# Expert tiles between the scores split one product early, look-up tables on ScalarE, the last V tiles in other buffers, and the output by halves

## The chip, the cores and the metric

The kernel runs on one core of a Trainium2 chip. The metric is the device time of one execution in microseconds. Work is done by five engines that each run their own instructions in order: TensorE (matrix products), VectorE, ScalarE, GpSimd and SyncE (which issues most of the DMAs).

## The reference, cut to what matters

One encoder layer over 512 tokens of width 1024. The part around the change is the expert layer (PEER) and the final norm:

```python
q = (ht @ w_q).reshape(T, PEER_HEADS, 2, PEER_HALF_DIM)
s1 = jnp.einsum('thd,hkd->thk', q[:, :, 0], keys[:, 0])
s2 = jnp.einsum('thd,hkd->thk', q[:, :, 1], keys[:, 1])
v1, i1 = lax.top_k(s1, PEER_TOPK)          # 16 of 128 keys, in each half
v2, i2 = lax.top_k(s2, PEER_TOPK)
cand = (v1[..., :, None] + v2[..., None, :]).reshape(T, PEER_HEADS, 256)
sc, ci = lax.top_k(cand, PEER_TOPK)
idx = i1[ci // 16] * 128 + i2[ci % 16]     # look-ups along the last axis
gates = jax.nn.softmax(sc, axis=-1)
...
a = einsum('chkd,cd->chk', U[idx], h2)     # 16384 experts, 8 heads x 16 each
w = gelu(a) * gates
x = x + gate2 * einsum('chk,chkd->cd', w, V[idx])
return rmsnorm(x, g_final)
```

Before it come the adaLN modulation, attention, a gated MLP and their output projection, which the change doesn't touch.

## The kernel before

Tokens lie in four blocks of 128. For blocks 0 to 2 (384 tokens) the experts are computed densely: the 16384 experts are 128 tiles of 128, tile e gives a 128 x 384 product with U (`a_mm`, 24 products into one accumulator, then Gelu in `a_gelu`), is multiplied with a gate matrix, and goes into six accumulators `outs` (three blocks by two halves of 512 columns) with 18 products. Block 3 (`GB`) is computed by gathering its experts' rows; its route and its gathers are a list `fill` of small steps that is spread over the main loop by costs written beside them.

A float32 product is made of three products of split operands (`mm3`): each weight is split into a high part on ScalarE and a low part on VectorE (`split_into`, lines 77 and 78). `a_load` loads and splits an expert tile: raw tiles in the three buffers tagged `ur`, high and low parts in two each, `uh` and `ul`. V tiles use two buffers `vr` and two each of `vh` and `vl`; the last two tiles' parts already lie in `uh` and `ul`.

The stages around the change, in order of time:

- **Scores and routing** (from about 270 us). For each of eight heads `score` makes two query products and their key scores (`q`, `qT`, `sc`, `s`). Then come the expert tiles of that head (one each, nine behind the last), and then VectorE's key search of the head (`route_keys`). After each four heads a group is routed: `route_cands`, `route_pick`, `route_decode`, and two times `route_lookup`, which finds `i1[ci // 16]` and `i2[ci % 16]` without a gather: a one-hot mask of 12 x 16 x 16 values by a comparison (line 593), times the table of indices (line 595), summed by halves (lines 597 and 599).
- **Gate build** (about 467 to 608 us). For 48 steps of eight tokens, one-hot matrices are made on VectorE and ScalarE, multiplied on TensorE (`gg`), and stored. The order of TensorE, ScalarE and VectorE is written out by hand (`manual_schedule`), and twelve expert tiles (18 to 29) are woven in through the list `todo`.
- **Main loop** over e = 0 to 127. The U product runs `AHEAD` = 30 tiles ahead of the V product. The V products of the last four tiles (`TAIL`) are held and done together.
- **Output.** For each block: times `gate2`, plus the residual, sum of squares (ScalarE's Square), times `g_final`, root on GpSimd, scale on ScalarE, and two DMAs from SyncE's queue. Its tiles `yf` share the tag `ur`.

Outside the parts written by hand the framework's planner fixes the order of each engine's instructions before the run: what comes first in the program has precedence, and what is ready by its own estimate may go ahead of what is not. A tile waits for a buffer of its tag. So loads and small steps can stand far from their place in the program.

Of the kernel before, what the change touches and what calls it, by code (L numbers as in the profile page):

```python
# [9 lines left out]
F32 = mybir.dt.float32  # L10
F32R = mybir.dt.float32r
BF16 = mybir.dt.bfloat16
# [7 lines left out]
P = 128  # L20
# [37 lines left out]
def tile_kernel(ctx: ExitStack, tc: tile.TileContext, a: dict, out: bass.AP):  # L58
# [506 lines left out]
    def route_decode(r):  # L565
        pl, tag, ci = r["pl"], r["tag"], r["ci"]
        n = r["nb"] * r["nh"]
        rt_ = lambda m, dt=F32: pl.tile([P, n, K], dt, name=f"{m}{tag}", tag=m, bufs=1)
        t3, t2 = rt_("t3", U32), rt_("t2", U32)
        nc.vector.tensor_single_scalar(t3, ci, 3, op=ALU.logical_shift_right)  # L570
        nc.vector.tensor_single_scalar(t2, ci, 2, op=ALU.logical_shift_right)
        row, st, u = rt_("row"), rt_("rst"), rt_("ru")
        rcf = pl.tile([P, 2, n, K], BF16, name=f"rcf{tag}", tag="rcf", bufs=1)
        nc.vector.scalar_tensor_tensor(row, t3, 5.0, t2, op0=ALU.add, op1=ALU.max)
        nc.vector.scalar_tensor_tensor(row, row, 42.0, ci, op0=ALU.add, op1=ALU.max)
        nc.vector.tensor_scalar(row, row, -48.0, 0.0, op0=ALU.add, op1=ALU.max)
        nc.vector.tensor_copy(rcf[:, 0], row)
        nc.vector.tensor_scalar(st, row, 7.0, 8.0, op0=ALU.mult, op1=ALU.add)
        nc.vector.tensor_scalar(u, row, 3.0, 24.0, op0=ALU.mult, op1=ALU.add)
        nc.vector.scalar_tensor_tensor(st, row, 15.0, st, op0=ALU.mult, op1=ALU.min)  # L580
        nc.vector.scalar_tensor_tensor(st, u, 48.0, st, op0=ALU.min, op1=ALU.min)
        nc.vector.tensor_add(st, st, row)
        nc.vector.tensor_sub(rcf[:, 1], ci, st)
        i12f = pl.tile([P, n, 2, K], BF16, name=f"i12f{tag}", tag="i12f", bufs=1)
        nc.vector.tensor_copy(i12f, r["i12"].rearrange("p b h f k -> p (b h) f k"))
        r["rcf"], r["i12f"] = rcf, i12f

    def route_lookup(r, f, dst):

        n = r["nb"] * r["nh"]  # L590
        sh = [P, n, K, K]
        oh = r["pl"].tile(sh, BF16, name=f"oh{r['tag']}{f}", tag="oh", bufs=2)
        nc.vector.tensor_tensor(oh, r["rcf"][:, f].unsqueeze(2).to_broadcast(sh),
                                jrep.unsqueeze(1).to_broadcast(sh), op=ALU.is_equal)
        nc.vector.tensor_tensor(oh, oh, r["i12f"][:, :, f, :].unsqueeze(3).to_broadcast(sh), op=ALU.mult)
        for w in (8, 4, 2):
            nc.vector.tensor_add(oh[:, :, :w, :], oh[:, :, :w, :], oh[:, :, w:2 * w, :])
        o5 = oh.rearrange("p (b h) j k -> p b h j k", h=r["nh"])
        nc.vector.tensor_add(dst, o5[:, :, :, 0, :], o5[:, :, :, 1, :])
# [13 lines left out]
    with ExitStack() as qs:  # L613
# [78 lines left out]
        ahead = FIRST  # L692
        score(0)
        r = None
        for h in range(PH):
            if h + 1 < PH:
                score(h + 1)
            while ahead < FIRST + h + 1 + (LATE if h == PH - 1 else 0):
                dense_a(ahead)
                ahead += 1  # L700
            s_sb = scores.pop(h)
            hl = h % HG
            if hl == 0:
                r = route_tiles(R, f"d{h}", ND, HG)
            for b in range(ND):
                for f in range(2):
                    route_keys(r, b, hl, f, s_sb[:, b, f, :])
            if hl == HG - 1:
                hs = slice(h - HG + 1, h + 1)
                route_cands(r)  # L710
                for b in range(ND):
                    for i in range(HG):
                        route_pick(r, b, i, sca[:, b, h - HG + 1 + i, :])
                route_decode(r)
                for f, dst in ((0, i1a), (1, i2a)):
                    route_lookup(r, f, dst[:, :, hs, :])
        route_gates(R, sca, gts, ND * PH)

    flat = lambda t, b: t.rearrange("p b h k -> p b (h k)")[:, b, :]
# [3 lines left out]
    with ExitStack() as gs:  # L723
# [63 lines left out]
        for k in range(nu):  # L787
            e = ahead + k
            s0 = k * NG // nu
            st = {}  # L790
            todo[s0].append(lambda e=e, st=st: st.update(hl=a_load(e)))
            for c in range(KD):
                def part(e=e, st=st, c=c):
                    if c == 0:
                        st["p"] = a_psum(e)
                    a_mm(e, st["p"], st["hl"], c)
                todo[s0 + 2 + c * NG // nu // KD].append(part)
            todo[s0 + 3 + NG // nu].append(lambda e=e, st=st: a_gelu(e, st["p"]))
# [66 lines left out]
    for h in range(PH):  # L865
        for f in range(2):
            fill.append((1.6, lambda h=h, f=f: route_keys(st["r"], 0, h, f, st["sg"][:, 2 * h + f, :])))
    fill.append((1.2, lambda: route_cands(st["r"])))
    for h in range(PH):
        fill.append((1.3, lambda h=h: route_pick(st["r"], 0, h, st["sc"][:, 0, h, :])))  # L870
    fill.append((4.0, lambda: route_decode(st["r"])))
    for f in range(2):
        fill.append((5.0, lambda f=f: route_lookup(st["r"], f, st["i"][f])))
    fill.append((1.2, lambda: route_gates(st["R"], st["sc"], gtg, PH)))
    fill.append((0.3, gb_idx))
    for n in range(NS):
# [11 lines left out]
    for e in range(NE):  # L888
        if e + AHEAD < NE:
            dense_a(e + AHEAD)  # L890
        if e == 0:
            gt = g0
        elif e % GE == 0:
            gt = wp.tile([P, NTC, GE, TC], F32, name=f"g{e}", tag="g", bufs=2)
            nc.sync.dma_start(gt, gd[e // GE])
        vraw = vp.tile([P, D], F32, name=f"v{e}r", tag="vr", bufs=2)
        nc.sync.dma_start(vraw, a["peer_v"][e * P:(e + 1) * P, :])
        if e < NE - 2:
            vh = vp.tile([P, D], F32R, name=f"v{e}h", tag="vh", bufs=2)
            vl = vp.tile([P, D], F32R, name=f"v{e}l", tag="vl", bufs=2)  # L900
        else:
            vh = up.tile([P, D], F32R, name=f"v{e}h", tag="uh", bufs=2)
            vl = up.tile([P, D], F32R, name=f"v{e}l", tag="ul", bufs=2)
        nc.scalar.copy(vh, vraw)
        last = nc.vector.tensor_sub(vl, vraw, vh.bitcast(F32))
        w = a_tiles.pop(e)
        wv3 = w.rearrange("p (c t) -> p c t", t=TC)
        nc.vector.tensor_tensor(wv3, wv3, gt[:, :, e % GE, :], op=ALU.mult)  # L908
        wh = wp.tile([P, TD], F32R, name=f"w{e}h", tag="wh", bufs=TAIL)
        wl = wp.tile([P, TD], F32R, name=f"w{e}l", tag="wl", bufs=TAIL)  # L910
        split_into(wh, wl, w)
        held.append((e, wh, wl, vh, vl))
        if e < NE - TAIL or e == NE - 1:
            for b in range(ND):
                bs = slice(b * P, (b + 1) * P)
                for e_, wh, wl, vh, vl in held:
                    for hf in range(2):
                        sl = slice(hf * 512, (hf + 1) * 512)
                        mm3(outs[2 * b + hf], (wh[:, bs], wl[:, bs]), (vh[:, sl], vl[:, sl]),
                            e_ == 0, e_ == NE - 1)  # L920
            held.clear()
        due += slack[e] * rate
        with tc.issue_after(last.ins):
            while fill and (due >= fill[0][0] or e == NE - 1):
                cost, fn = fill.pop(0)
                fn()
                due -= cost
# [2 lines left out]

    gfin = gp.tile([P, D], F32, name="gfin", tag="g", bufs=4)
    nc.sync.dma_start(gfin, a["g_final"].partition_broadcast(P))
    for b in (GB, 0, 1, 2):
        if b in (GB, 0):
            xr = gp.tile([P, D], F32, name=f"xr{b}", tag="g", bufs=4)
        else:
# [1 line left out]
        nc.sync.dma_start(xr, x2d[b * P:(b + 1) * P, :])  # L938
        y = up.tile([P, D], F32, name=f"yf{b}", tag="ur", bufs=3)
        ss = gp.tile([P, 2], F32, name=f"ssf{b}", tag="ssf", bufs=2)  # L940
        for hf in range(2):
            sl = slice(hf * 512, (hf + 1) * 512)
            nc.vector.tensor_mul(y[:, sl], accg[:, sl] if b == GB else outs[2 * b + hf], gate2[:, sl])
            nc.vector.tensor_add(y[:, sl], y[:, sl], xr[:, sl])
            nc.scalar.activation(xr[:, sl], y[:, sl], AF.Square, accum_out=ss[:, hf:hf + 1])
            nc.vector.tensor_mul(y[:, sl], y[:, sl], gfin[:, sl])
        nc.vector.tensor_add(ss[:, 0:1], ss[:, 0:1], ss[:, 1:2])
        r = rstd_of(ss[:, 0:1], D, f"fin{b}")
        for hf in range(2):
            sl = slice(hf * 512, (hf + 1) * 512)  # L950
            nc.scalar.activation(y[:, sl], y[:, sl], AF.Copy, scale=r[:, 0:1])
            nc.sync.dma_start(out[b * P:(b + 1) * P, sl], y[:, sl])


def arrays_of(i):
# [59 lines left out]
```

## Time and profile before

| | us |
|---|---|
| median of 3 runs | 1567.22 (1566.68 to 1567.84) |
| the profiled execution, its own time | 1570.06 |
| its span, first to last instruction | 1568.3 |
| TensorE busy | 1492.6 |
| VectorE busy | 1240.9 |
| ScalarE busy | 636.6 |
| mean granted clock of TensorE, share of full | 0.981 |

The span is what the profile shows; the execution's own time has the 1.76 us around it too. Busy times overlap, since the engines work side by side. In the profile PE is TensorE's products, PEld its weight loads, DVE is VectorE, ACT ScalarE, POOL GpSimd, SP SyncE; a q behind a name is that engine's queue, and L595 is line 595 of the kernel.

### The profile page before, as it was taken

To read this page: it belongs to the slowest core of one execution; us is meant where nothing else is said; L and a number is where in the kernel's file an instruction comes from. 1 tells how busy PE (TensorE), PEld (TensorE's weight loads), DVE (VectorE), ACT (ScalarE), POOL (GpSimd) and SP (SyncE) were. 2 spreads that over 40 slices of the span, in tenths; PEclk is the share of its full clock that TensorE was granted. 3 is DMA by queue.
4 is the path that set the end of the run, shared out by engine and by line. 5 is a ranking of instruction groups with operands and counts; after the bars stand their busy time and mean duration, and the time that the engine had idled before them with its cause. 6 is when DMAs were issued, how large, how long until landed. Compare 5 with 4: busy or idle time off the path is not lost.

```text
span 1568.3 us, 21451 instructions
## 1 busy us (share of the span) xinstructions
PE 1492.6 (95%) x7675; PEld 1317.9 (84%) x7675; DVE 1240.9 (79%) x2388; ACT 636.6 (41%) x1092; POOL 397.1 (25%) x335
## 2 busy tenths in 40 slices
PE   2899999998979999999999999999999999999996
PEld 1765787887879999999999999999999999998884
DVE  6937865579989997987887878878888888886774
ACT  2533434432338997334333333333333333332343
POOL 1202100000000000002554444444544544542210
PEclk9899999999999999999999999999999999999998
DMA  9626334331325769666999999988999998987873
GB/s 366 232 79 223 130 132 148 112 104 48 101 94 159 237 211 300 218 224 220 354 351 319 321 330 328 326 318 318 336 330 314 326 325 315 333 287 230 256 237 121
DMA packets 147226, 380.71 MB, mean 243 GB/s; under 512 B 11184, under 2 KB 59840, under 8 KB 146864
## 3 DMA queue, kind: packets, MB, share of 16 engines
q1 hardware_dynamic: 103472, 221.02, 40.5%
q0 software_dynamic: 42352, 153.62, 28.7%
q10 hardware_dynamic: 1296, 4.72, 0.8%
q8 instruction: 60, 0.98, 0.2%
q14 instruction: 46, 0.38, 0.1%
HBM read 349.16 MB, written 30.15 MB: 242 GB/s over the span
## 4 chain that ended last, share of the span: by engine, by line
PE 86%; DVE 7%; DMA 3%; ACT 1%; issue 1%; POOL 0%; SPq 0%; ACTq 0%; POOLq 0%; DVEq 0%
PE out L83 11%; PE out L84 11%; PE out L82 11%; PE pa L82 11%; PE pa L84 11%; PE pa L83 11%; PE gg L770 5%; DMA wada<-w_ada 2%; PE q L82 1%; PE q L84 1%; PE q L83 1%; PE yo L82 1%; PE yo L84 1%; PE yo L83 1%; DVE macc L149 1%
## 5 line engine op out<-in xcount | busy, mean ns | idle before, releaser
L842 POOL DMA_INDIRECT gu<-peer_u,idx x128 | 181.3, 1417 | 653.6 <-DVE w17l L78 467.6
L842 POOL DMA_INDIRECT gv<-peer_v,idx x128 | 173.0, 1351 | 235.0 <-DVE accg L862 209.0
L850 DVE SCALAR_TENSOR_TENSOR scr<-gu,h2g 128x1024 bf16<-128x1024 f32 x128 | 156.5, 1222 | 24.1 <-DMA gu<-peer_u,idx 21.8
L862 DVE SCALAR_TENSOR_TENSOR accg<-gv,wg,accg 128x1024 f32<-128x1024 f32 x127 | 162.8, 1282 | 7.1 <-DMA gv<-peer_v,idx 4.6
L770 PE MATMUL gg<-o,o 128*128 128x128 f32 x768 | 96.0, 280 | 3.6 <-ACT o L764 2.0
L770 PEld LDWEIGHTS gg<-o,o 128*128 128x128 f32 x768 | 94.6, 196 | 4.1 <-ACT o L764 4.1
L908 DVE TENSOR_TENSOR a<-a,g 128x384 f32<-128x384 f32 x128 | 69.1, 550 | 6.4 <-DMA g<-gd 2.9
L764 ACT ACTIVATE o<-o1b,gT 128x128 f32<-128x128 bf16 x192 | 63.4, 405 | 13.8 <-DVE o1b L751 7.2
L518 ACT ACTIVATE a<-pa 128x384 f32<-128x384 f32 x128 | 61.7, 483 | 13.2 <-PE pa L84 13.2
L149 DVE SCALAR_TENSOR_TENSOR macc<-wada,csil,macc 128x1024 f32<-128x1024 f32 x40 | 51.2, 1280 | 9.5 <-DMA wada<-w_ada 9.1
L753 DVE TENSOR_TENSOR o<-iota_s,gT 128x1024 f32<-128x1024 f32 x48 | 58.4, 1216 | 0.3 <-PE gg L770 0.2
L757 DVE TENSOR_SCALAR o<-iota_s,gT 128x128 f32<-128x128 f32 x192 | 53.2, 339 | 0.0
L779 ACT COPY st<-gg 128x512 f32<-128x512 f32 x96 | 50.5, 581 | 0.0
L159 PE MATMUL mcol<-ident_s,macc 128*128 128x128 f32 x32 | 7.4, 391 | 26.6 <-DVE macc L146 23.1
L135 POOL DMA_DIRECT2D wada<-w_ada x32 | 17.1, 535 | 59.9 <-DVE macc L149 24.3
L159 PEld LDWEIGHTS mcol<-ident_s,macc 128*128 128x128 f32 x32 | 5.5, 201 | 28.3 <-DVE macc L146 17.9
L424 ACT ACTIVATE pe<-s,mx 128x512 f32<-128x512 f32 x16 | 11.0, 688 | 28.4 <-DVE mx L422 20.8
L684 PE MATMUL sc<-keys_s,qT 128*128 128x128 f32 x128 | 18.1, 284 | 2.8 <-ACT qT L681 2.8
L751 DVE TENSOR_TENSOR o1b<-erep,gB 128x512 bf16<-128x512 bf16 x48 | 20.0, 416 | 0.9 <-ACT gB L734 0.9
L684 PEld LDWEIGHTS sc<-keys_s,qT 128*128 128x128 f32 x128 | 15.6, 191 | 5.7 <-ACT qT L681 4.3
L531 DVE MAX8 v12d<-s 128x8 f32<-128x128 f32 x48 | 12.7, 280 | 9.4 <-ACT s L686 9.4
L431 PEld LDWEIGHTS o<-vv,pts 128*128 128x128 f32 x128 | 16.1, 192 | 2.3 <-DVE mx L422 0.8
(2789 smaller groups left out, 4952.2 us busy)
## 6 DMA issues: line engine op xcount, KB each, us to landing
gd<-st SPq DMA_DIRECT2D x12, 1984.0 KB, 7.9
g<-gd SPq DMA_DIRECT2D x31, 768.0 KB, 8.4
wada<-w_ada POOLq DMA_DIRECT2D x32, 512.0 KB, 4.7
wada<-w_ada SPq DMA_DIRECT2D x16, 512.0 KB, 10.1
x<-x SPq DMA_DIRECT2D x4, 512.0 KB, 12.4
x<-x ACTq DMA_DIRECT2D x4, 512.0 KB, 3.8
x2d<-x ACTq DMA_DIRECT2D x4, 512.0 KB, 2.8
gu<-peer_u,idx POOLq DMA_INDIRECT x128, 7.3
```

The lines of the kernel that those rows point to most:

```text
L82: nc.tensor.matmul(o, lhsT=lh, rhs=rh, start=first, stop=False)
L83: nc.tensor.matmul(o, lhsT=lh, rhs=rl, start=False, stop=False)
L84: nc.tensor.matmul(o, lhsT=ll, rhs=rh, start=False, stop=last)
L149: nc.vector.scalar_tensor_tensor(acc, w, csil[:, c:c + 1], acc, op0=ALU.mult, op1=ALU.add)
L518: nc.scalar.activation(t, p[:, :TD], AF.Gelu)
L753: nc.vector.tensor_tensor(o2s[n], iota.unsqueeze(1).to_broadcast([P, UT, P]), tT[:, 1, t0:t0 + UT].unsqueeze(2).to_broadcast([P, UT, P]), ...
L764: nc.scalar.activation(o1s[n][:, i, :], e[:, :, i], AF.Copy, scale=tT[:, 2, t0 + i:t0 + i + 1])
L770: nc.tensor.matmul(pgs[n][i // 4][:, i % 4 * P:(i % 4 + 1) * P], lhsT=o2[:, i, :], rhs=o1[:, i, :], start=True, stop=True)
L842: nc.gpsimd.indirect_dma_start(out=g, out_offset=None, in_=src, in_offset=bass.IndirectOffsetOnAxis(ap=idx[:, s:s + 1], axis=0))
L850: nc.vector.scalar_tensor_tensor(scr, g, 1.0, st["h2g"], op0=ALU.mult, op1=ALU.mult, accum_out=actg[:, n:n + 1])
L862: nc.vector.scalar_tensor_tensor(accg, g, wg[:, s:s + 1], accg, op0=ALU.mult, op1=ALU.add)
L908: nc.vector.tensor_tensor(wv3, wv3, gt[:, :, e % GE, :], op=ALU.mult)
```

## The change

Four edits in one.

- *Expert tiles.* The loop between the scores loads and splits tile e + 1 right behind the products of tile e, before that tile's Gelu and before the key search. The first tile of the gate build (18) is so loaded and split in the routing stage.
- *Look-up tables.* The cast of the indices to bf16 moves from VectorE to ScalarE (`route_tables`). `route_rep` makes on ScalarE a dense copy of the index table, repeated 16 times along the last axis, and the multiply reads this copy in place of the broadcast. There is one buffer for the copy and, instead of two, one for the mask. The costs in `fill` are adapted.
- *Last V tiles.* The raw tiles of e = 125, 126 and 127 take the tag `ur`.
- *Output.* The held products of a block finish its first half before its second. The output works by halves in an order written by hand for blocks 0 to 2: one half is multiplied by `g_final` into a tile `yg` ahead of the root and scaled by ScalarE, the other gets root and gain in one VectorE operation, and each half has its own queue, ScalarE's and SyncE's.

```diff
+    def route_tables(r):
         i12f = pl.tile([P, n, 2, K], BF16, name=f"i12f{tag}", tag="i12f", bufs=1)
-        nc.vector.tensor_copy(i12f, r["i12"].rearrange("p b h f k -> p (b h) f k"))
-        r["rcf"], r["i12f"] = rcf, i12f
+        nc.scalar.copy(i12f, r["i12"].rearrange("p b h f k -> p (b h) f k"))
+    def route_rep(r, f):
+        n = r["nb"] * r["nh"]
+        t = r["pl"].tile([P, n, K, K], BF16, name=f"rep{r['tag']}{f}", tag="rep", bufs=1)
+        nc.scalar.copy(t, r["i12f"][:, :, f, :].unsqueeze(3).to_broadcast([P, n, K, K]))
+        r["rep"][f] = t
...
-        oh = r["pl"].tile(sh, BF16, name=f"oh{r['tag']}{f}", tag="oh", bufs=2)
+        oh = r["pl"].tile(sh, BF16, name=f"oh{r['tag']}{f}", tag="oh", bufs=1)
...
-        nc.vector.tensor_tensor(oh, oh, r["i12f"][:, :, f, :].unsqueeze(3).to_broadcast(sh), op=ALU.mult)
+        nc.vector.tensor_tensor(oh, oh, r["rep"].pop(f), op=ALU.mult)
...
+        nxt = a_load(ahead)
...
-                dense_a(ahead)
+                hl, nxt = nxt, None
+                p = a_psum(ahead)
+                for c in range(KD):
+                    a_mm(ahead, p, hl, c)
+                nxt = a_load(ahead + 1)
+                a_gelu(ahead, p)
...
+                route_tables(r)
+                route_rep(r, 0)
                 route_cands(r)
...
-                for f, dst in ((0, i1a), (1, i2a)):
-                    route_lookup(r, f, dst[:, :, hs, :])
+                route_lookup(r, 0, i1a[:, :, hs, :])
+                route_rep(r, 1)
+                route_lookup(r, 1, i2a[:, :, hs, :])
...
-            todo[s0].append(lambda e=e, st=st: st.update(hl=a_load(e)))
+            if k:
+                todo[s0].append(lambda e=e, st=st: st.update(hl=a_load(e)))
+            else:
+                st.update(hl=nxt)
...
+    fill.append((0.0, lambda: (route_tables(st["r"]), route_rep(st["r"], 0))))
...
-    fill.append((4.0, lambda: route_decode(st["r"])))
-    for f in range(2):
-        fill.append((5.0, lambda f=f: route_lookup(st["r"], f, st["i"][f])))
+    fill.append((3.6, lambda: route_decode(st["r"])))
+    fill.append((4.0, lambda: route_lookup(st["r"], 0, st["i"][0])))
+    fill.append((0.0, lambda: route_rep(st["r"], 1)))
+    fill.append((4.0, lambda: route_lookup(st["r"], 1, st["i"][1])))
...
-        vraw = vp.tile([P, D], F32, name=f"v{e}r", tag="vr", bufs=2)
+        if e < NE - 3:
+            vraw = vp.tile([P, D], F32, name=f"v{e}r", tag="vr", bufs=2)
+        else:
+            vraw = up.tile([P, D], F32, name=f"v{e}r", tag="ur", bufs=3)
...
-                for e_, wh, wl, vh, vl in held:
-                    for hf in range(2):
-                        sl = slice(hf * 512, (hf + 1) * 512)
-                        mm3(outs[2 * b + hf], (wh[:, bs], wl[:, bs]), (vh[:, sl], vl[:, sl]),
-                            e_ == 0, e_ == NE - 1)
+                for hf, (e_, wh, wl, vh, vl) in [(hf, h) for hf in range(2) for h in held]:
+                    sl = slice(hf * 512, (hf + 1) * 512)
+                    mm3(outs[2 * b + hf], (wh[:, bs], wl[:, bs]), (vh[:, sl], vl[:, sl]),
+                        e_ == 0, e_ == NE - 1)
...
+    def o_sum(b, hf):
+        (xr, y, ss, yg), sl = outp[b], halves[hf]
+        nc.vector.tensor_mul(y[:, sl], accg[:, sl] if b == GB else outs[2 * b + hf], gate2[:, sl])
+        nc.vector.tensor_add(y[:, sl], y[:, sl], xr[:, sl])
+        nc.scalar.activation(xr[:, sl], y[:, sl], AF.Square, accum_out=ss[:, hf:hf + 1])
+
+    def o_gain(b):
+        xr, y, ss, yg = outp[b]
+        nc.vector.tensor_mul(yg, y[:, halves[0]], gfin[:, halves[0]])
...
+    def o_store(b):
+        (xr, y, ss, yg), r = outp[b], rs[b][:, 0:1]
+        nc.scalar.activation(yg, yg, AF.Copy, scale=r)
+        nc.vector.scalar_tensor_tensor(y[:, halves[1]], y[:, halves[1]], r, gfin[:, halves[1]],
+                                       op0=ALU.mult, op1=ALU.mult)
+        nc.scalar.dma_start(out[b * P:(b + 1) * P, halves[0]], yg)
+        nc.sync.dma_start(out[b * P:(b + 1) * P, halves[1]], y[:, halves[1]])
...
+    with tc.manual_schedule(engines={nc.vector.engine, nc.scalar.engine}):
+        for b in range(ND):
+            o_sum(b, 0)
+            if b:
+                o_store(b - 1)
+            o_gain(b)
+            o_sum(b, 1)
+            o_root(b)
+        o_store(ND - 1)
```

## Rows read from the trace of the kernel before

**Rows 1.** The page's first part: busy time, share of the span and instructions of each engine.
```profile
PE 1492.6 (95%) x7675; PEld 1317.9 (84%) x7675; DVE 1240.9 (79%) x2388; ACT 636.6 (41%) x1092; POOL 397.1 (25%) x335
```

**Rows 2.** Stretches: busy us (instructions) per engine, PEclk the granted clock, DMA share, GB/s.
```profile
368.00:384.00 16.00, 12.21 (x66) 10.28 (x65) 16.00 (x22) 4.83 (x10) 0.00 (x0) 1.00 0.03 9
384.00:400.00 16.00, 13.40 (x54) 10.39 (x54) 15.22 (x88) 3.57 (x6) 0.00 (x0) 0.89 0.10 34
...
448.00:464.00 16.00, 13.72 (x63) 13.72 (x64) 13.12 (x14) 1.93 (x3) 0.00 (x0) 0.79 0.30 98
...
520.00:560.00 40.00, 40.00 (x312) 40.00 (x311) 39.21 (x90) 36.89 (x96) 0.00 (x0) 1.00 0.76 234
...
1200.00:1400.00 200.00, 200.00 (x1005) 182.06 (x1004) 164.43 (x163) 69.42 (x96) 95.06 (x67) 1.00 0.90 321
```

**Rows 3.** Waits of TensorE, 256 to 482 us: us in total, times, longest us.
```profile
PE q L84 <- DVE wq12l L78: 2.8, 1, 2.8
PE sc L684 <- ACT qT L681: 2.8, 2, 1.4
```

**Rows 4.** The tiles of the two look-ups: xcount, ns min/median/max, first and last start, forms.
```profile
L593 DVE TENSOR_TENSOR ohd<-rcfd,jrep x4: 1746/1748/1752, 369.2 to 453.2; 128x3072 bf16<-128x3072 bf16 x4
L595 DVE TENSOR_TENSOR ohd<-ohd,i12fd x4: 3346/3348/3350, 371.1 to 459.5; 128x3072 bf16<-128x3072 bf16 x4
...
L585 DVE CAST i12fd<-i12d x2: 352/352/352, 354.2 to 438.2; 128x384 bf16<-128x384 uint32 x2
```

**Rows 5.** Timeline of ScalarE: start us, us, engine line op out<-in xcount [idle before <-releaser].
```profile
342.90 1.05 ACT L77 CAST wq9h<-wq9r 128x1024 fp32r<-128x1024 f32 x1 [4.60 <-PE q L83]
343.86 0.58 ACT L681 COPY qT<-q 128x512 f32<-128x512 f32 x1
```

**Rows 6.** Timeline where the last head's scores arrive and the gate build starts, VectorE, then TensorE.
```profile
416.64 0.49 DVE L531 MAX8 v12d<-s 128x8 f32<-128x128 f32 x2 [3.64 <-ACT s L686]
...
465.53 0.36 DVE L599 TENSOR_TENSOR i2a<-ohd 128x192 f32<-128x192 bf16 x1
...
470.32 1.22 DVE L78 TENSOR_TENSOR u18l<-u18r,u18h 128x1024 fp32r<-128x1024 f32 x1 [0.63 <-ACT u18h L77]
...
473.16 1.19 PE L770 MATMUL gg<-o,o 128*128 128x128 f32 x4 [1.63 <-DVE o L753]
```

**Rows 7.** Waits of ScalarE, 256 to 482 us.
```profile
ACT u17h L77 <- PE pa L83: 10.6, 1, 10.6
```

**Rows 8.** Timeline of TensorE at the end, then two pieces of the chain that ended last.
```profile
1531.87 0.39 PE L82 MATMUL out<-v123h,w123h 128*128 128x512 f32 x1
...
1535.95 0.39 PE L82 MATMUL out<-v124h,w124h 128*128 128x512 f32 x1
...
1552.95 0.40 PE L84 MATMUL out<-v127h,w127l 128*128 128x512 f32 x1
...
1538.67 3.79 DMA v127r<-peer_v
```

**Rows 9.** Timeline of the output at the end (SPq: SyncE's queue), then DMA issues: xcount, KB, us.
```profile
1518.20 1.28 DVE L943 TENSOR_TENSOR yf<-accg,gate 128x512 f32<-128x512 f32 x2
...
1552.26 9.53 SPq L952 DMA_DIRECT2D out_dram<-yf  x6
...
1555.33 0.68 DVE L944 TENSOR_TENSOR yf<-yf,xr 128x512 f32<-128x512 f32 x1
...
1557.68 0.61 ACT L945 ACTIVATE xr<-yf 128x512 f32<-128x512 f32 x1
...
1558.42 0.69 DVE L946 TENSOR_TENSOR yf<-yf,gfin 128x512 f32<-128x512 f32 x1 [1.54 <-ACT xr L945]
...
1559.52 0.54 POOL L114 TENSOR_TENSOR fin_r<-fin_ms,nhalf 128x1 f32<-128x1 f32 x1 [3.11 <-DVE fin_ms L112]
1560.10 1.33 ACT L951 ACTIVATE yf<-yf,fin_r 128x512 f32<-128x512 f32 x2 [1.71 <-POOL fin_r L114]
...
out_dram<-yf SPq DMA_DIRECT2D x8, 256.0 KB, 2.1
```

More of the change, by code (lines that the diff above doesn't have):

```diff
@@ L583, in route_decode @@
         nc.vector.tensor_sub(rcf[:, 1], ci, st)
+        r["rcf"] = rcf
+    def route_tables(r):
+        pl, tag = r["pl"], r["tag"]
+        n = r["nb"] * r["nh"]
         i12f = pl.tile([P, n, 2, K], BF16, name=f"i12f{tag}", tag="i12f", bufs=1)
-        nc.vector.tensor_copy(i12f, r["i12"].rearrange("p b h f k -> p (b h) f k"))
-        r["rcf"], r["i12f"] = rcf, i12f
+        nc.scalar.copy(i12f, r["i12"].rearrange("p b h f k -> p (b h) f k"))
+        r["i12f"] = i12f
+        r["rep"] = {}
+    def route_rep(r, f):
+        n = r["nb"] * r["nh"]
+        t = r["pl"].tile([P, n, K, K], BF16, name=f"rep{r['tag']}{f}", tag="rep", bufs=1)
+        nc.scalar.copy(t, r["i12f"][:, :, f, :].unsqueeze(3).to_broadcast([P, n, K, K]))
+        r["rep"][f] = t
     def route_lookup(r, f, dst):
@@ L932, in tile_kernel, with o_load @@
     nc.sync.dma_start(gfin, a["g_final"].partition_broadcast(P))
-    for b in (GB, 0, 1, 2):
+    halves = [slice(hf * 512, (hf + 1) * 512) for hf in range(2)]
+    outp = {}
+    def o_load(b):
         if b in (GB, 0):
@@ L940, in tile_kernel @@
         ss = gp.tile([P, 2], F32, name=f"ssf{b}", tag="ssf", bufs=2)
[L941 to L946, printed above, removed]
-        nc.vector.tensor_add(ss[:, 0:1], ss[:, 0:1], ss[:, 1:2])
@@ L948, in tile_kernel @@
[L948 to L952, printed above, removed]
+        yg = gp.tile([P, 512], F32, name=f"yg{b}", tag="yg", bufs=2)
+        outp[b] = (xr, y, ss, yg)
+    def o_sum(b, hf):
[3 more added lines that the diff above has]
+        nc.scalar.activation(xr[:, sl], y[:, sl], AF.Square, accum_out=ss[:, hf:hf + 1])
@@ new lines, in o_gain, with o_root @@
+    def o_gain(b):
+        xr, y, ss, yg = outp[b]
+        nc.vector.tensor_mul(yg, y[:, halves[0]], gfin[:, halves[0]])
+    rs = {}
+    def o_root(b):
+        ss = outp[b][2]
+        nc.vector.tensor_add(ss[:, 0:1], ss[:, 0:1], ss[:, 1:2])
+        rs[b] = rstd_of(ss[:, 0:1], D, f"fin{b}")
+    def o_store(b):
[5 more added lines that the diff above has]
+        nc.sync.dma_start(out[b * P:(b + 1) * P, halves[1]], y[:, halves[1]])
@@ L955, in arrays_of @@
+    for b in (GB, 0, 1, 2):
+        o_load(b)
+        if b == GB:
+            o_sum(b, 0)
+            o_gain(b)
+            o_sum(b, 1)
+            o_root(b)
+            o_store(b)
+    with tc.manual_schedule(engines={nc.vector.engine, nc.scalar.engine}):
+        for b in range(ND):
+            o_sum(b, 0)
+            if b:
+                o_store(b - 1)
+            o_gain(b)
+            o_sum(b, 1)
+            o_root(b)
+        o_store(ND - 1)
 def arrays_of(i):
```

## The prediction

> **What bounds the kernel now.** I read the page's engine line first, then the stretches, then the waits of the stretches that are not full, and last the timelines of the two places where TensorE runs dry. TensorE is busy for 95% of the span and VectorE for 79% [rows 1], but these are averages over stages. In the gate build and in the main loop TensorE is busy for the whole stretch at the full clock, 40.00 of 40 us and 200.00 of 200 us [rows 2]. There VectorE and ScalarE have room, and what is taken from them gives nothing; only the number of products counts, and the change leaves that as it is. So the change can pay in two places: between the scores and the first gate product, and after the last V tiles.
>
> In the routing stage VectorE is the bound. From 368 to 384 us it is busy for 16.00 of 16 us while TensorE has 12.21, then 13.40 of the next 16 at a mean granted clock of 0.89 [rows 2]. TensorE's longest wait there is 2.8 us for the low half of the twelfth query weight, which stands on VectorE behind the first look-up group [rows 3]. The second group does the same at 448 to 464: TensorE 13.72 of 16, clock 0.79 [rows 2]. From the last head's scores at 416.64 to the last look-up sum, which ends at 465.9, VectorE works through one chain, and the gate build can't start before it [rows 6].
>
> **The change part by part, against the profiled run of 1570.06 us (span 1568.3).**
>
> *Look-up tables.* Each look-up multiplies its comparison mask by a table that is broadcast along the innermost axis: 3348 ns. The comparison before it has the same 3072 bf16 elements, with every operand dense along that axis: 1748 ns [rows 4]. The new multiply reads a dense bf16 copy, so its nearest row is the comparison. I take 1.75 us, a saving of 1.6; the other bound is 3.35, a saving of nothing. The 0.35 us cast [rows 4] goes to ScalarE. A group of two look-ups so loses 2 x 1.6 + 0.35 = 3.5 us on VectorE, and there are two groups.
>
> First group: the low half that TensorE awaits comes 3.5 us sooner, more than the 2.8 that it waited, so that wait goes. A mean of 0.89 over 16 us, between 2.4 GHz and 1.2, is 3.5 us at the lower level, which cost 1.8 us of work; with no wait before it I expect no fall. Gain 4.6 us on the scores of the last head (bounds 0 and 5.3). VectorE, 3.5 us lighter and with 3.64 us idle before those scores [rows 6], keeps up.
>
> Second group: VectorE's chain to the gates is 3.5 us shorter. The mask now has one buffer, so the second comparison can't be slipped between the first look-up's sums. I take 0.5 us off for hand-overs between dependent operations; the bound is a small operation's 0.36 us [rows 6] for each of five hand-overs in two look-ups, 3.6, which would leave nothing. Gain 3.0.
>
> The copies: ScalarE takes 1.05 us for 1024 elements and 0.58 for 512 [rows 5], 0.92 ns an element, so 3072 take 2.9 us. Four in the routing, and two of 2048 elements (2.0 us) in the main loop for the last token block. I cost them at nothing: ScalarE is busy for 4.83, 3.57 and 1.93 of 16 us around the groups and 69 of 200 in the main loop [rows 2]. The first copy of a group needs only the key indices and is ready before the candidates. The second waits until the first multiply lets the one buffer go, and meanwhile VectorE has the sums and the second comparison to do, about 3.7 us, against 2.9. Without that cover each copy costs up to 2.9.
>
> The Trainium skill says the reverse of this edit: its page ScalarE: Activation LUTs, section Rules for kernel authors, wants multiplies and adds on VectorE, there up to three times as fast per element in bf16. By it the four copies would be 11.7 us spent for 6.4 saved. The rows show whose time it is: ScalarE's is idle here.
>
> *Expert tiles one product early.* The splits of tiles 8 and 9 move ahead of a head's key search. Nothing new runs; TensorE gets tile products for its two 1.4 us waits for the query copy [rows 3]. That work comes out of a later stretch that VectorE bounds, so the gain is indirect: tile 10's split (1.22 us, as tile 18's) can fall into VectorE's 3.64 us idle time [rows 6]. I take 1.0, bounds 0 and 2.8. Also, tile 18's split leaves the gate build, where it stands ahead of the second step: 1.22 us and 0.63 of waiting for its high half, after which TensorE waits 1.63 for its one-hots [rows 6]. I take 1.4 (bounds 0 and 1.9); after that TensorE sets the pace.
>
> *Last V tiles.* Tile 127 is loaded only when tile 125 is split, at 1538.67, and lands 3.79 us later [rows 8]. In the expert tiles' buffers, which are free once the last expert tile is split, the last three loads need not wait. TensorE's 72 held products run from 1535.95 to 1553.35, 17.4 us, where the eighteen before took 4.08 [rows 8], so 16.3 for 72. I take 0.9 of the 1.1, since tile 125's split still needs a buffer that tile 123 holds. The bound below is nothing.
>
> *Output by halves.* From TensorE's end at 1553.35 to the end of the last issue (1552.26 + 9.53 = 1561.79 [rows 9]) it is 8.4 us: the last block's sums stand behind the block before, and two scalings of 0.67 run in series. New: all of half 0 is done while TensorE works on half 1, since that takes 12 products, 2.7 us. Then for half 1: multiply 0.68, add 0.68, Square 0.61 and its reading 0.19, the way to the root 0.5 (1558.39 to 1559.52, less the multiply of 0.69 that stood between, 0.61 from issue to issue), the root 0.54, one scaling of 0.69 on each of two engines at once, the issue 0.36, and 0.15 for hand-overs: 4.4 [rows 9]. It saves 4.0. But now two halves of 256 KB land together, where one takes 2.1 us [rows 9]; between 0 and 2.1 more, I take 0.7. With the 0.9 the end gains 4.2 (bounds 0.7 and 5.1).
>
> The Trainium skill, DMA: Bandwidth & Descriptors, section Issuing engines are not separate DMA queues, says that DMAs of several engines share the same 16 engines, so that a second issuer saves its issue time alone. By it my 0.7 stays; if it were wrong, the sum would be 0.7 better. No row of before shows two issuers at once at the end.
>
> *At nothing.* The lighter fill list of the main loop: TensorE hides it [rows 2]. Half before tile in the held products: the same 72.
>
> **Sum.** 4.6 + 3.0 + 1.0 + 1.4 + 4.2 = 14.2 us. From 1570.06 that is 1555.9; the median of the runs stands 2.8 below the profiled run, so I forecast 1567.2 - 14.2 = 1553.0 us.
>
> **The rivals.** *The second copy is late.* It may stand on ScalarE behind the gates' table switches and a cast, and VectorE then waits up to 2.5 us in each group; the first group's wait comes back in part. That takes 5: 1558.0. For it: one buffer for the copies. Against it: ScalarE's idle time.
>
> *The multiply gets no faster.* Then the groups save 0.35 each: 0.7 + 1.0 + 1.4 + 4.2 = 7.3, 1559.9. Against it: the comparison's row [rows 4].
>
> *The gathered block's output moves to the end.* Its result tile shares the three buffers that V tiles now take. At 1518.20 it hides in the main loop [rows 9]; behind tile 125's split, its 4.1 us on VectorE (four of 0.64, two of 0.65, small ones) would delay the last block by some 3.5: 1556.5.
>
> *Slower: a convoy on ScalarE.* Engines run in order. If a copy is queued behind an expert tile's cast that waits for TensorE to free a buffer, VectorE's multiply waits for the copy, and the next split that TensorE needs stands behind the multiply. The longest such cast waits 10.6 us [rows 7]. Caught once, the sum is 1563.6; caught in both groups, 1553.0 + 21.2 = 1574.2. It decides from 14.2 us of stall on. For it: the casts have precedence over the copies. Against it: the casts' usual wait is 4.60 [rows 5], and a copy fits inside. It is here that the rule of the Trainium skill's page ScalarE: Activation LUTs would be borne out.
>
> **How the numbers follow.** Forecast 0.60 (own range 1549 to 1557), late copy 0.16, multiply no faster 0.05, gathered block late 0.08, convoy once 0.05, twice 0.06. All bounds at their best give 20 us, 1547. The range 1547 to 1561 leaves out the convoys and a little. A measurement of this kernel can tell about 0.2%, 3.1 us, from no change: faster below 1564.1, which holds the first four cases and most of the fifth, 0.88; the rest of the fifth and part of the last, same 0.06; slower 0.06.
>
> **What would show it.** Right: multiplies of about 1.75 us; no TensorE wait for the twelfth weight's low half and a clock of 1.00 from 384 to 400; the last look-up sum near 457; the second gate step under 4 us after the first; TensorE's last product about 10 us earlier than 1553; the last issue within 5 us of it. Wrong: a ScalarE copy of over 3 us or behind a long wait, or a main loop where TensorE is not full, where nothing in my sum looks.

## The result, and the profile after

The changed kernel takes 1551.37 us (median of 6 runs, 1550.02 to 1553.27) where the kernel before took 1567.51 beside it: ratio 0.9896, 95% interval 0.9885 to 0.9907, so 16.1 us faster. The forecast was 14.2 us and 1553.0. One of the six executions of the kernel before, at 7608 us, has no part in the ratio. The profiled execution took 1551.62 us with a span of 1549.8.

Of the 18.5 us between the two spans (1568.3 less 1549.8) 2.3 have nothing to do with the change. The first query product, with nothing changed ahead of it, starts at 279.25 us before and at 276.95 after; over the profiles of this study that start lies between 274.6 and 279.4, early (up to 277.0) where the granted clock from 40 to 80 us was 0.96 to 1.00, and late (from 277.8) where it was 0.83 to 0.85. So I compare stages by three marks that every trace has: the first query product (A), the last head's copy of its scores (B), the first product of V tile 124 (C), and the end of the span.

| kernel | A to B | B to C | C to end |
|---|---|---|---|
| before | 136.88 | 1119.82 | 32.35 |
| after | 130.44 | 1113.75 | 28.66 |

That is 6.4 + 6.1 + 3.7 = 16.2 us, which agrees with the runs. The forecast's sum, cut the same way, was 4.6, then 3.0 + 1.0 + 1.4 = 5.4, then 4.2. After, run a second time beside other kernels, gave 130.39, 1113.89 and 28.64: here the stages repeat within 0.2 us.

TensorE is busy for 1485.2 us after, 96% of the span, where [rows 1] have 1492.6 and 95%: the work hardly changes, the waits do.

Three stretches of after, columns as in [rows 2]. From 384 to 400 us TensorE went from 13.40 at clock 0.89 to 15.98 at 1.00. From 448 to 464, where the gate build now starts, it is emptier and slower than before, when this stretch was still routing.

```profile
384.00:400.00 16.00, 15.98 (x84) 13.55 (x83) 16.00 (x83) 4.02 (x8) 0.00 (x0) 1.00 0.25 75
...
448.00:464.00 16.00, 10.00 (x54) 9.63 (x55) 14.44 (x30) 8.36 (x26) 0.00 (x0) 0.68 0.10 34
480.00:520.00 40.00, 40.00 (x312) 40.00 (x312) 39.20 (x89) 36.47 (x95) 0.00 (x0) 1.00 0.72 222
```

TensorE's waits of after in the same stretch as [rows 3]. The wait for the twelfth weight is gone, and the two for the query copy fell from 2.8 to 0.9. A new one, for the last look-up sum, is the longest.

```profile
PE gt L752 <- DVE i2a L612: 4.8, 1, 4.8
...
PE sc L697 <- ACT qT L694: 0.9, 2, 0.7
```

The look-up's multiply and the copy that it reads, after (ns min/median/max), against [rows 4]: 1754 ns for 3348. The Trainium skill, VectorE: DVE Perf Modes, section What auto-detection actually checks, says that in an operation with two sources VectorE takes two elements a cycle if every tensor is 16-bit with a step of one; the broadcast operand has no such step, the copy has, and the trace agrees.

```profile
L608 DVE TENSOR_TENSOR ohd<-ohd,repd x4: 1749/1754/1759, 368.7 to 448.2; 128x3072 bf16<-128x3072 bf16 x4
...
L598 ACT COPY repd<-i12fd x4: 2738/2752/2752, 351.1 to 440.9; 128x3072 bf16<-128x3072 bf16 x4
```

The timeline of after where the gate build starts, against [rows 6]. TensorE has nothing to do until the last sum, and the first 32 gate products then take 6.56 us, where 16 take 1.95 a little later: they run at half clock (granted clock 0.50 from 455.54 to 461).

```profile
452.02 0.36 DVE L612 TENSOR_TENSOR i2a<-ohd 128x192 f32<-128x192 bf16 x1
...
455.54 6.56 PE L792 MATMUL gg<-o,o 128*128 128x128 f32 x32 [1.57 <-ACT o L786]
...
462.98 1.95 PE L792 MATMUL gg<-o,o 128*128 128x128 f32 x16
```

The timeline of after at the end, against [rows 8, 9]. Tile 125's split is VectorE's last split; its first output multiply follows at 1526.17, with TensorE less than a third through the held products (5.0 of 17.1 us), and the last block's second half starts at 1538.37, just after TensorE's last product. The last issue ends at 1542.39 + 0.37 = 1542.76, 4.5 us after TensorE (8.4 before). From there to the end of the span it is 7.0 us, 6.5 before.

```profile
1522.61 1.23 DVE L935 TENSOR_TENSOR v125l<-v125r,v125h 128x1024 fp32r<-128x1024 f32 x1 [0.39 <-ACT v125h L934]
1526.17 0.69 DVE L979 TENSOR_TENSOR yf<-out,gate 128x512 f32<-128x512 f32 x1 [2.34 <-PE out L84]
...
1537.82 0.40 PE L84 MATMUL out<-v127h,w127l 128*128 128x512 f32 x1
...
1538.37 0.68 DVE L979 TENSOR_TENSOR yf<-out,gate 128x512 f32<-128x512 f32 x1
...
1542.39 0.37 ACTq L999 DMA_DIRECT2D out_dram<-yg  x1
```

### The profile page after: what moved, and what is told of

It is laid out like the page before. It is cut to its first block, busy times and chain, and to the rows that moved or that the text cites. A ratio compares the mean times of both kernels' runs of the same rounds, so it can differ in the third digit from the quotient of the medians.

```text
span 1549.8 us, 21464 instructions
## 1 busy us (share of the span) xinstructions
PE 1485.2 (96%) x7675; PEld 1311.7 (85%) x7675; DVE 1234.8 (80%) x2385; ACT 649.1 (42%) x1097; POOL 393.5 (25%) x335
## 4 chain that ended last, share of the span: by engine, by line
PE 85%; DVE 8%; DMA 3%; issue 2%; ACT 1%; POOL 0%; SPq 0%; POOLq 0%; DVEq 0%; ACTq 0%
PE out L84 11%; PE out L83 11%; PE out L82 11%; PE pa L84 11%; PE pa L83 11%; PE pa L82 11%; PE gg L792 6%; DMA wada<-w_ada 2%; PE q L82 1%; PE q L83 1%; PE q L84 1%; DVE macc L149 1%; PE yo L83 1%; PE yo L84 1%; PE yo L82 1%
## 5 line engine op out<-in xcount | busy, mean ns | idle before, releaser
L867 POOL DMA_INDIRECT gu<-peer_u,idx x128 | 178.0, 1391 | 641.2 <-PE out L83 443.3
L135 POOL DMA_DIRECT2D wada<-w_ada x32 | 17.1, 535 | 60.7 <-DVE macc L149 25.5
L418 PE MATMUL s<-kr,qr 64*128 64x512 f32 x32 | 18.0, 641 | 0.0
```

The source lines that it names most:

```text
L867: nc.gpsimd.indirect_dma_start(out=g, out_offset=None, in_=src, in_offset=bass.IndirectOffsetOnAxis(ap=idx[:, s:s + 1], axis=0))
```

## The experiments

**Each edit alone.** Four kernels, each the kernel before with one of the four edits of the diff above and nothing else. Theory A: the four act in four places and add up.

```diff
tiles_only:  -                dense_a(ahead)
             +                nxt = a_load(ahead + 1)
lookup_only: -        nc.vector.tensor_tensor(oh, oh, r["i12f"]... op=ALU.mult)
             +        nc.vector.tensor_tensor(oh, oh, r["rep"].pop(f), op=ALU.mult)
output_only: -    for b in (GB, 0, 1, 2): ...
             +    with tc.manual_schedule(...): o_sum, o_store, o_gain, o_sum, o_root
vtiles_only: +            vraw = up.tile([P, D], F32, name=f"v{e}r", tag="ur", bufs=3)
```

> The kernel before with the early expert tiles alone; look-ups, V tiles and output as before. Theory A, the four edits act in four places and add up: the two waits for the query copy shrink (1.9 us) and the gate build starts without tile 18's split (1.3 us), so 2 to 4 us faster than before, about 3.2. Theory B, VectorE bounds the routing with its old look-ups, so that an earlier split only moves the same VectorE work: within 1 us of before, and the 2.8 us wait for the twelfth weight's low half stays or grows.

> The kernel before with the look-up tables on ScalarE alone; the expert tiles are split as before. Theory A: the last head's scores come 4.6 us sooner (no wait for the twelfth weight, no half clock at 384 to 400 us) and the chain from them to the last look-up sum is 4.8 us shorter: 8.5 to 10 us faster than before, about 9.4, and the waits for the query copy stay at 2.8 us in two. Theory B, the lighter VectorE pays only together with the early tiles, since without them TensorE falls dry at other weights or copies: under 7 us faster, with a new wait of 2 us or more among TensorE's waits before 420 us.

> The kernel before with the output by halves and the held products half before tile, nothing else. Theory A: TensorE's end to the end of the last issue shrinks by 3.9 us and the last landing grows by 0.5: 3.0 to 3.8 us faster than before, about 3.4. Theory B, the two halves that land together cost what the second queue saves, or the half order holds TensorE up at the last V tile: under 2 us faster.

> The kernel before with the last three V tiles in the expert tiles' buffers, nothing else. Theory A, from the trace after the change: 0.3 us faster, which a measurement can't tell from no change, and the 72 held products take 17.1 us. Theory B, the prediction's: 0.9 us faster, 72 products in 16.5. Theory C, in the old output the gathered block's result waits for a buffer and moves to the end: 3 us slower.

| kernel | ratio to before, 95% | A to B | B to C | C to end |
|---|---|---|---|---|
| tiles_only | 0.9986 (0.9977 to 0.9994) | 136.90 | 1116.39 | 32.00 |
| lookup_only | 0.9970 (0.9958 to 0.9981) | 136.84 | 1114.26 | 31.99 |
| output_only | 1.0016 (1.0007 to 1.0025) | 136.88 | 1120.01 | 33.27 |
| vtiles_only | 0.9989 (0.9980 to 0.9998) | 138.11 | 1118.45 | 29.72 |

The ratios sum to a gain of 6.1 us (0.14 + 0.30 - 0.16 + 0.11 = 0.39% of 1567.7), the stages to 11.4 (3.8 + 6.0 - 1.1 + 2.8), neither to 16. Theory A is out. The marks say where: neither the early tiles nor the look-ups bring the last head's scores (A to B) any sooner, and the output by halves alone is slower. The runs of each kernel show 1 to 1.6 us less than its stages; the marks leave out the first 280 us, but whether all of that gap lies there was not settled. None of the four expectations had the output by halves alone slower, or the V tiles alone worth the 1.7 us that their runs show.

*Scores.* With the early tiles alone the wait for the twelfth weight stays. This is a line of TensorE's waits in that kernel.

```profile
PE q L84 <- DVE wq12l L78: 2.8, 1, 2.8
```

With the look-ups alone it is gone, but a longer one takes its place, and the clock still falls (to 0.50 in the 4.1 us behind that wait). A line of that kernel's waits of TensorE, one of its stretches, and one of VectorE's timeline.

```profile
PE pa L84 <- DVE u8l L78: 4.3, 1, 4.3
```
```profile
384.00:400.00 16.00, 11.57 (x52) 9.74 (x51) 14.74 (x79) 4.66 (x10) 0.00 (x0) 0.82 0.10 34
```
```profile
394.65 1.21 DVE L78 TENSOR_TENSOR u8l<-u8r,u8h 128x1024 fp32r<-128x1024 f32 x1
```

Tile 8's low half is split at 394.65, in the middle of the next head's key search. In the changed kernel it is split ahead of that search, as a line of its VectorE timeline shows. TensorE's next stop stood right behind the one removed.

```profile
385.24 1.22 DVE L78 TENSOR_TENSOR u8l<-u8r,u8h 128x1024 fp32r<-128x1024 f32 x1
```

The waits for the query copy fall to 0.9 us with the look-ups alone too, against the expectation; with the tiles alone 1.4 stay.

*End.* In the kernel before tile 127's low half, split at 1543.57, is what lets the first half of any block be complete. VectorE's first output multiply follows it, and all three blocks' output then runs on VectorE one after another; TensorE's end is not what it waits for. Three lines of VectorE's timeline of before, which the prediction does not name.

```profile
1543.57 1.23 DVE L905 TENSOR_TENSOR v127l<-v127r,v127h 128x1024 fp32r<-128x1024 f32 x1 [3.29 <-ACT v127h L904]
1545.76 1.29 DVE L943 TENSOR_TENSOR yf<-out,gate 128x512 f32<-128x512 f32 x2 [0.96 <-PE out L84]
...
1559.29 0.15 DVE L112 TENSOR_SCALAR fin_ms<-ssf 128x1 f32<-128x1 f32 x1
```

The output by halves behind the same late tile: its VectorE timeline. From the first multiply to the end of the last block's sum (line 112) the three blocks take 1544.33 to 1558.91 + 0.15 = 1559.06, 14.7 us, where the old order took 13.7 (1545.76 to 1559.29 + 0.15). From that sum to the end of the last issue it is 0.5 us less (1.85 for 2.35), from there to the end of the span 0.6 more (7.1 for 6.5), and the first multiply stands 0.2 nearer to C. That makes the 0.9 us by which this kernel's end is longer.

```profile
1542.03 1.23 DVE L905 TENSOR_TENSOR v127l<-v127r,v127h 128x1024 fp32r<-128x1024 f32 x1 [2.69 <-ACT v127h L904]
1544.33 0.69 DVE L949 TENSOR_TENSOR yf<-out,gate 128x512 f32<-128x512 f32 x1 [1.08 <-PE out L84]
...
1558.91 0.15 DVE L112 TENSOR_SCALAR fin_ms<-ssf 128x1 f32<-128x1 f32 x1
```

The stages of vtiles_only also show the spread of a single profile: A to B is 1.2 us longer and B to C 1.4 shorter than before, with no edit of the routing or the gate build. TensorE's waits up to B are the same (2.8, 2.8 and 1.0); what differs is the granted clock, 0.83 from 100 to 120 us behind A where before has 0.91, and 0.91 from 160 to 200 us behind A where before has 0.83.

**In pairs.** From these I formed theory B: the edits work in two pairs, each of which removes two waits in a row.

```diff
tiles_lookup:  the edits of tiles_only and lookup_only on the kernel before
vtiles_output: the edits of vtiles_only and output_only on the kernel before
```

> The kernel before with the early tiles and the look-up tables together; V tiles and output as before. Theory B (formed from the single parts: neither alone brought the last head's scores any sooner, since the early tiles alone keep the 2.8 us wait for the twelfth weight and the look-ups alone only turn it into 4.3 us for tile 8's low half): together 6.4 us on the scores and 6 us from there to the held products, so 12 to 13 us faster than before, with no TensorE wait over 1 us between 290 and 440 us. Theory A, the parts add: 3 to 4 plus 5 to 6, that is 8 to 9.5 us faster.

> The kernel before with the V tiles and the output by halves together; tiles and look-ups as before. Theory B: the old end is set by tile 127's late low half, after which VectorE works through all three blocks' output; the V tiles lift that, and only then does the output by halves stand at TensorE's end: 3 to 4.5 us faster than before, TensorE's end to the end of the last issue 4.5 us. Theory A, the parts add as they measured alone (2.3 faster, 2.5 to 3 slower): no difference, within 1 us.

| kernel | ratio to before, 95% | A to B | B to C | C to end |
|---|---|---|---|---|
| tiles_lookup | 0.9931 (0.9917 to 0.9945) | 130.39 | 1113.67 | 31.96 |
| vtiles_output | 0.9972 (0.9961 to 0.9983) | 136.91 | 1119.93 | 28.70 |

Theory B holds, stage by stage: the first pair brings the whole 6.5 us on the scores and 6.2 behind them, the second the whole 3.7 at the end. The runs of tiles_lookup show 10.8 us (0.69%) of the 13.0 that its stages show. Why they fall short by 2 us was not settled; it may be the spread of the first 280 us. Behind the scores the two edits overlap instead: alone 3.4 and 5.6, together 6.2.

**The gate build's start.** After the change TensorE runs dry for 4.8 us and then runs at half clock. Three kernels on the changed one go for that place: *late9* does tile 18's products there, *v01_late* takes two V splits out of VectorE's chain to the last look-up sum, *v01_late9* does both.

```diff
-LATE = 8
+LATE = 9
...
+        if e < 2:
+            with tc.issue_after(routed.ins):
+                last = nc.vector.tensor_sub(vl, vraw, vh.bitcast(F32))
```

> The changed kernel with tile 18's products ahead of the gate transposes (ten tiles behind the last head instead of nine). It fills the 4.8 us in which TensorE waits for the last look-up sum. Theory C, TensorE bounds the gate build: 4.1 us of products (24 of 0.17) leave a full stretch for an empty one, and the first 32 gate products no longer run at half clock (6.6 us instead of 3.9): 4 to 7 us faster than the changed kernel, 20 to 23 faster than before. Theory D, VectorE, 98% busy in the gate build, bounds it as much as TensorE: only the 2.7 us of the clock or less, 16 to 19 faster than before.

> late9, and the low-half splits of V tiles 0 and 1 (two of 1.2 us on VectorE, which stand in the routing chain) queued behind the last look-up sum. If the chain of VectorE to that sum sets the gate build's start, 1 to 2.4 us faster than late9; if the splits only move into the gate build, where VectorE is 98% busy, the same as late9 within 0.5 us, or slower by up to 2.4.

> The changed kernel, nine tiles behind the last head as there, and the low-half splits of V tiles 0 and 1 queued behind the last look-up sum. If VectorE's chain sets the gate build's start, the sum ends 2.4 to 3 us earlier and TensorE waits 2 us for it instead of 4.8; of this the two splits take 2.4 back in the gate build if VectorE bounds it (no more than 0.6 faster than the changed kernel), or nothing if TensorE does (2.4 to 3 faster).

> The changed kernel once more, beside the others on the same chip: 15.5 to 16.5 us faster than before, and from the first query product to the last head's scores 130.4 us, from there to the first product of V tile 124 1113.8, from there to the end 28.7, as in its first profile. If these stages move by more than 0.5 us, the differences between the experiments are smaller than they look.

> The changed kernel with tile 18's products ahead of the gate transposes once more, to tell it from the changed kernel in the same call: 1 to 2 us faster than that if the 1.6 us between the last scores and V tile 124 that its profile shows are real, no difference if they are the spread of the profiles.

| kernel | ratio to before, 95% | A to B | B to C | C to end |
|---|---|---|---|---|
| late9 | 0.9890 (0.9875 to 0.9905) | 130.44 | 1112.11 | 28.67 |
| late9_again | 0.9894 (0.9879 to 0.9909) | 130.39 | 1112.26 | 28.68 |
| v01_late9 | 0.9897 (0.9882 to 0.9912) | 130.41 | 1112.81 | 28.71 |
| v01_late | 0.9892 (0.9877 to 0.9907) | 130.37 | 1113.00 | 28.65 |
| after_again | 0.9894 (0.9879 to 0.9909) | 130.39 | 1113.89 | 28.64 |

The stretches of late9 show the wait filled and the full clock, and where it went.

```profile
448.00:464.00 16.00, 12.79 (x90) 12.12 (x91) 15.02 (x31) 9.04 (x27) 0.00 (x0) 1.00 0.22 67
480.00:520.00 40.00, 39.44 (x306) 38.76 (x305) 39.29 (x89) 36.92 (x96) 0.00 (x0) 1.00 0.69 215
```

The gate build has lost its full TensorE stretches (39.44 of 40 us, where after has 40.00): with less to do TensorE runs short, while VectorE is as busy as it was (39.29 for 39.20). That fits theory D, by which both engines bound that stage: of the 4 to 7 us 1.6 remain, in both profiles of late9. The runs can't tell them from nothing: late9_again 1551.19 us, after_again 1550.60. Taking the V splits out of the chain brings the last look-up sum 2.0 us closer to the last scores in v01_late (447.54 less 404.95, for 451.07 less 406.47 in after_again), but B to C is only 0.9 shorter, and on late9 they bring nothing (1112.81). The two splits now stand between the last sum and the first one-hots, at 447.81 and 449.28, and TensorE's long wait moves on to these. A line of TensorE's waits in v01_late.

```profile
PE gg L792 <- DVE o L775: 3.3, 1, 3.3
```

The first 32 gate products then take 6.46 us, at half clock as in the changed kernel. No version here is measurably faster than the changed kernel.

**Whose time the copies cost.** The changed kernel with the cast and the copies on VectorE.

```diff
-        nc.scalar.copy(i12f, r["i12"].rearrange("p b h f k -> p (b h) f k"))
+        nc.vector.tensor_copy(i12f, r["i12"].rearrange("p b h f k -> p (b h) f k"))
-        nc.scalar.copy(t, r["i12f"][:, :, f, :].unsqueeze(3).to_broadcast([P, n, K, K]))
+        nc.vector.tensor_copy(t, r["i12f"][:, :, f, :].unsqueeze(3).to_broadcast([P, n, K, K]))
```

> The changed kernel with the cast of the indices and the four dense copies on VectorE instead of ScalarE. Theory E, it is ScalarE's idle time that pays: VectorE, the bound of both look-up groups, gets 0.35 and two copies of 1.75 to 3.35 us (the dense and the broadcast multiply) more in each group, 3.9 to 7.1, so the last head's scores and the last look-up sum come later by that much each: 5 to 14 us slower than the changed kernel, 2 to 11 faster than before. Theory F, by the Trainium skill's rule (ScalarE: Activation LUTs, Rules for kernel authors) VectorE does in bf16 what ScalarE does in up to three times the time: by it a copy takes about 0.9 us in place of 2.75, ScalarE's waits of up to 5 us for the buffer no longer matter, and it is the same as the changed kernel or slower by 4 at most.

The ratio to before is 0.9957 (0.9943 to 0.9971): 1560.04 us against 1550.60 of after_again, 9.4 more. A to B is 131.88, B to C 1119.67, C to end 28.65: 1.5 and 5.8 us more than after_again. That is 7.3 us by the stages, for work of 4 x 1.755 + 2 x 0.35 = 7.7 on VectorE. Part of the wait for the twelfth weight comes back too (1.3 us). The copy in this kernel, by its tile.

```profile
L598 DVE COPY repd<-i12fd x4: 1754/1755/1757, 351.8 to 447.3; 128x3072 bf16<-128x3072 bf16 x4
```

This is theory E: here VectorE's time is the kernel's time and ScalarE's is not, although VectorE does the copy 1.57 times as fast (1755 ns for 2752). The Trainium skill's rule (ScalarE: Activation LUTs, section Rules for kernel authors), which is stated for additions and multiplications, with a factor of up to about three in bf16, has the right direction for this one copy. The copy reads the same broadcast table that slowed the two-source multiply, and is not slowed by it: 3072 elements in 1755 ns, as the dense multiply.

## Why the prediction was right, and where its steps were not

The total held (14.2 us forecast, 16.1 measured, inside the range), and so did the places: routing, gate start, end. What failed is the sharing out of the gain among the edits, in four terms that balanced, so that the close total is partly luck: by place the forecast was 1.8 us short on the scores, 0.7 short behind them and 0.5 too high at the end.

- *Multiply 1.75 us, copies 2.9, hidden on ScalarE.* Right: 1.754 and 2.752. ScalarE waits 5.0 us in two for the one buffer, and no VectorE wait for a copy appears; the late copy, the unchanged multiply and the convoys did not happen.
- *First group 4.6 us from the look-ups.* The wait went and the clock rose as said, but the look-ups alone bring 0.0 there. The step that failed is "with no wait before it I expect no fall": it asked what is late next for VectorE ("keeps up") and not for TensorE, whose next low half, tile 8's, stood behind the key search. With the early tiles it is 6.4. The shorter waits for the query copy (2.8 less 0.9) are 1.9 of that; the prediction put them down to the tiles, but the look-ups alone bring them.
- *Early tiles 1.0 us indirect, 1.4 at the gate.* Mis-sized and misplaced: alone 0.0 on the scores and 3.4 behind them, and the condition for the 6.4. With the second group's 3.0 they were to give 5.4 behind the scores; measured were 6.1, and 5.6 with the look-ups alone. That TensorE would then wait 4.8 us for the last look-up sum and drop to half clock was not foreseen; filling the wait brought 1.6 us in late9's profiles. The prediction gives VectorE room in the gate build, but its own row there has VectorE busy for 39.21 of 40 us [rows 2].
- *V tiles 0.9 us, by TensorE's held products.* The 72 products went from 17.4 to 17.1 us only (1521.14 to 1538.22). Yet the edit alone brings 2.6 us at the end (32.35 to 29.72). The prediction had tile 127's landing in its rows [rows 8] and priced it by TensorE; its price was VectorE's output chain, which starts with it.
- *Output 4.0 us, landing 0.7.* Alone 0.9 slower; behind the V tiles 1.0 better (29.72 to 28.70). The working took TensorE's end as the start of the last block's sums; before, VectorE, begun late, was still busy with the blocks ahead of it. The V tiles alone cut the way from TensorE's end to the end of the last issue from 8.4 to 6.2 us (1549.83 to 1555.98 in vtiles_only), so 2.3 of the 4.0 were theirs. Both edits together give 3.7 where 4.2 was said. The landing cost 0.5 of the 0.7 (7.04 less 6.51), which is in line with the Trainium skill, DMA: Bandwidth & Descriptors, section Issuing engines are not separate DMA queues; no run here separates it from other causes.
- *The gathered block's output* stayed in the main loop: VectorE's list after 1517.6 us holds only the three dense blocks' output.
- *Two of its sums don't come out.* The best bounds that it names add to 18.6 us (5.3 + 3.5 + 2.8 + 1.9 + 5.1), not 20, and the chances of its first four cases to 0.89, which with most of the fifth is more than its 0.88. Neither touches the forecast.

## What to carry to other kernels

When a wait is removed, follow the same engine to the next operand that it needs and price that stop too: two edits that each bring nothing on a stage brought 6.5 us there together, and a list of gains per edit then has the right sum only by luck. At the end of a kernel, ask which operand lets the first output begin, not only when the last product ends. And an operation is cheap on the engine that has time, even where it takes 1.6 times as long.

## What the runs showed of the hardware

- The first 280 us, which no edit here touches, end anywhere between 274.6 and 279.4 us, with TensorE's granted clock from 40 to 80 us between 0.83 and 1.00. That spread is about as large as what the best of the four edits brought alone in the runs (4.7 us), and it is why single spans were not compared.
- After its 4.8 us wait TensorE ran most of the first 32 gate products at the lower of its two levels (1.2 GHz, granted clock 0.50 up to 461; 6.56 us, where 32 at the upper take 3.9), with only six short transposes and another 1.6 us of waiting between. In late9, with products in the wait's place, the clock of that stretch is 1.00.
